# Expert output projection deferred by one turn with TensorE's order written out, and the adaptive-norm matmuls spread over four column groups, in a two-layer trunk with mixture-of-experts

## The chip, the cores and the metric

The kernel runs on one core of a Trainium2 chip. The metric is device time in microseconds of one execution, the median of several. TensorE has two clock levels, 1.2 and 2.4 GHz; the profile gives the granted clock of a stretch as a share of the higher one.

## The reference

Two layers over 1,024 tokens of width 1,024. Layer 0 mixes with a gated delta rule and a sparse attention, layer 1 with a gated linear attention; after each mixer stands a mixture of experts. What the change touches is this:

```python
mod = cond @ ada_w[layer] + ada_b[layer]          # cond = silu(c): 1 x 1024, ada_w[layer]: 1024 x 6144
sh_m, sc_m, gt_m, sh_f, sc_f, gt_f = jnp.split(mod, 6, axis=-1)
...
def expert_block(args):                            # 32 experts a layer, 2 per token
    xi, e = args
    hid = jax.nn.silu(xi @ w1[e]) * (xi @ w3[e])   # w1, w3: 1024 x 512
    return hid @ w2[e]                             # w2: 512 x 1024
```

## The kernel before

All values are float32. A large matmul is made of three (`mm3`, lines 112 to 114): each operand is split into a rounded part "hi" and the remainder "lo" (both of type fp32r), and hi·hi, lo·hi and hi·lo are added up in PSUM.

**Adaptive norm** (`ada_steps`, line 282). The 6,144 columns of a layer are made in three rounds of 2,048. A round has 16 tiles of 128 rows by 1,024 columns (512 KB each). `cond` stands in TensorE as a stationary operand 32 columns wide, so a matmul fills 32 of the 128 columns of the array, and `tile_position=(0, q)` says which. A round's PSUM tile holds four strips of 512 values at partitions 0, 32, 64 and 96. One tile feeds two of them: `u` says which pair, and each of its two matmuls has 512 columns. The first round (layer 0, columns 0 to 2,047) loads its weights as eight wide tiles on SP before anything else can run (`first`, line 448), and its tiles come in pairs. The other five rounds (80 tiles, `later`, line 470) are loaded on POOL's queue into two buffers and are taken one tile at a time between the steps of the input projection (matmuls `pj`).

**Mixture of experts** (`moe`, lines 1401 to 1665), once per layer. Up to 128 tokens of an expert are gathered from DRAM on POOL (`fetch_tokens`, line 1474), turned by TensorE (`tokens`, `tp<-xg`, line 1485), and split by ScalarE (`xh`, line 1487) and VectorE (`xl`, line 1488). `up` is 24 matmuls of 512 columns for `w1` and 24 for `w3`. `gated` makes `silu(p1) * p3` (`s`, `hd`, line 1505). `hidden` turns that (`tp<-hd`, line 142) and splits it (`hh` on ScalarE, line 1513; `hl` on VectorE, line 1514). `down` is another 24 matmuls in two halves `u`, copied out by ScalarE (line 1532) and scattered by POOL (line 1521).

A weight of 2 MB comes from DRAM as two pieces of 1 MB on SP's queue (line 1442), into six buffers `raw`. Each piece is rounded by ScalarE (`mhi`, line 1430), and its remainder is made by VectorE (`mlo`, line 1431). There are four buffers for such a pair, so two weights at a time. In `up` the first piece serves the first 12 matmuls and the second the last 12; in `down` each half `u` needs the first piece for six matmuls and the second for the next six.

The loop's body writes, for expert e: `up` by w3, `gated`, `up` of e+1 by w1, `hidden`, the tokens of e+2, `down` by w2, scatter. Each engine runs its instructions strictly in its own program's order. That order is chosen when the program is built, by a scheduler that weighs estimated times; it moves instructions of all engines past each other where the data allow. Every fourth expert `find_places` computes the token places of four later experts (`ix`, lines 1460 and 1464).

Of the kernel before, what the change touches and what calls it, by code (L numbers as in the profile page):

```python
# [9 lines left out]
F32 = mybir.dt.float32  # L10
# [12 lines left out]
P = 128  # L23
# [51 lines left out]
def run(gen):  # L75
    for _ in gen:
        pass
# [10 lines left out]
class Trunk:  # L88
# [175 lines left out]
    def ada_steps(self, rounds, wp, pp, load, wait):  # L264


        nc, cp = self.nc, self.cp
        n, total = 0, 2 * KD * len(rounds)
        w = load(0)
        for layer, g in rounds:  # L270
            bias = wp.tile([P, 512], F32, name="adab", bufs=1)
            for j in range(4):
                q = g * 4 + j
                nc.scalar.dma_start(bias[32 * j:32 * j + 32], bcast(self.d["ada_b"][layer, q * 512:(q + 1) * 512], 32))
# [16 lines left out]
            if g:  # L291
                for j in range(4):
                    q = g * 4 + j
                    nc.scalar.dma_start(self.mods[layer, q * 512:(q + 1) * 512][None, :], mr[32 * j:32 * j + 1])
# [5 lines left out]
            nc.vector.tensor_copy(col, pt.rearrange("p (c j r) -> p j c r", c=4, j=4)[:, :, :, 0])  # L300
            self.COL[layer, g] = col

    def ada_tile(self, i, rounds):

        (layer, g), (k, u) = rounds[i // (2 * KD)], divmod(i % (2 * KD), 2)
        c0 = g * 2048 + u * 1024
        return self.d["ada_w"][layer, k * P:(k + 1) * P, c0:c0 + 1024]
# [110 lines left out]
    def even_inproj(self):  # L418
# [29 lines left out]
        def first(i):  # L448
            k, u = divmod(i, 2)
            if u == 0:  # L450
                wide[k] = wp.tile([P, KD * W], F32, name="aw", tag="wlo" if k % 2 else "whi", bufs=2)[:, :2048]
                nc.sync.dma_start(wide[k], d["ada_w"][0, k * P:(k + 1) * P, :2048])
            return wide[k][:, u * 1024:(u + 1) * 1024]

# [949 lines left out]
    def moe(self, layer):  # L1404
        nc, tc, d = self.nc, self.tc, self.d
        tt, ts, stt, act, mm, tr = self.tt, self.ts, self.stt, self.act, self.mm, self.tr
        with ExitStack() as st:
# [38 lines left out]
            def places(n, R, val, iy, it):  # L1446
# [8 lines left out]
                tt(ob, in16[:, :, :, None].to_broadcast(b4), self.iob[:, None, None, :].to_broadcast(b4), op=OP.is_equal)  # L1455
                tt(oa, oa, val[:, :, :, None].to_broadcast(a4), op=OP.mult)
                p = pp.tile([P, 512], F32, name="ix", bufs=1)
# [4 lines left out]
                act(t, p[:8, :n * 16], AF.Copy)  # L1462
                p = pp.tile([P, 512], F32, name="ix", bufs=1)
                mm(p[:, :n * 16], self.to8[:8], t, start=True, stop=True)
# [13 lines left out]
            def tokens(xg):  # L1478
                xh = sp.tile([P, KD, P], F32R, name="xh", bufs=2)
                xl = sp.tile([P, KD, P], F32R, name="xl", bufs=2)  # L1480
                for u in range(2):
                    p = pp.tile([P, 512], F32, name="tp", bufs=2)
                    for c in range(4):
                        k = u * 4 + c
                        tr(p[:, c * P:(c + 1) * P], xg[:, k * P:(k + 1) * P], self.ident)  # L1485
                    us = slice(u * 4, u * 4 + 4)
                    act(xh[:, us], as4(p), AF.Copy)  # L1487
                    tt(xl[:, us], as4(p), xh[:, us].bitcast(F32), op=OP.subtract)  # L1488
                return xh, xl

# [43 lines left out]
            def find_places(e, n):  # L1534
                es = slice(e, e + n)
                places(n, self.R[:, :, es], self.val[:, :, es], yix[:, es], tix[:, es])

            def fetch_tokens(e):
                return gather(tix[:, e:e + 1], xgs[e % 2])

            find_places(0, 2)
            g = fetch_tokens(0)
# [5 lines left out]
            with tc.issue_after(self.turned[-1].ins), tc.issue_after(self.added[-1].ins), tc.issue_after(found.ins):  # L1548
                w3 = weights(0, "exp_w3")
            xt = {0: tokens(xgs[0])}  # L1550
            fetch_tokens(1)
            p1 = up(xt[0], w1)
            find_places(2, 2)
            xt[1] = tokens(xgs[1])
            fetch_tokens(2)
            scat = []
            for e in range(NE):
# [17 lines left out]
                scat.append(s)  # L1575
                if e == 1:
# [35 lines left out]
            def pick():  # L1612
# [11 lines left out]
                nc.vector.tensor_copy(xh, xv)  # L1624
                places(1, ri[:, :, None], xh[:, :, None], ixn[:, 0:1], ixn[:, 1:2])
                gather(ixn[:, 1:2], xgs[0])
# [21 lines left out]
            with tc.For_i(0, nv, 1) as _:  # L1648
                scatter(y, ixc[:, 0:1])
                for n in range(2, 6):  # L1650
                    fetch(n)
                x = tokens(xgs[0])
                w1 = take(0)
# [442 lines left out]
```

## Time and profile before

| | |
|---|---|
| median of 3 runs | 3092.82 us (3088.14 to 3100.25) |
| the profiled execution | 3102.59 us, of which the profile's span is 3100.9 us |
| TensorE (PE) busy | 2698.4 us (87%) |
| VectorE (DVE) busy | 2213.0 us (71%) |
| ScalarE (ACT) busy | 1690.7 us (55%) |
| GpSimd (POOL) busy | 514.8 us (17%) |
| DMA | 683.08 MB, mean 220 GB/s |

PE is the matrix engine, PEld its weight loads, SPq the queue of DMAs that SP issues. `out<-in` names the tiles that an instruction writes and reads. In the profile a matmul's end is modelled, so consecutive matmuls overlap in the rows; what one costs in a row of many is the distance between starts. L with a number is a line of the kernel.

### The profile page before, as it was taken

What the parts mean: (1) busy time and instruction counts of PE and PEld (TensorE: products, weight loads), DVE (VectorE), ACT (ScalarE), POOL (GpSimd) and SP (SyncE); (2) the same over time, 40 slices, a digit from 0 to 9 for tenths busy, and PEclk for the clock granted to TensorE, in tenths of its full rate; (3) what the DMA queues carried; (4) which work ended last, traced back from release to release, by engine and by line L of the source; (5) the groups of instructions that cost most, each with busy time, mean ns of one, the idle gap of its engine ahead of it and who ended that gap; (6) DMA issues with size and microseconds to landing.
All of it is one profiled execution on the core that took longest, in us unless ns stands there. A gap on an engine that the chain in (4) does not pass through costs nothing. (4 is left out here: it accounts for less than half of the span.)

```text
span 3100.9 us, 46537 instructions
## 1 busy us (share of the span) xinstructions
PE 2698.4 (87%) x17606; PEld 2142.8 (69%) x17606; DVE 2213.0 (71%) x4033; ACT 1690.7 (55%) x2191; POOL 514.8 (17%) x511
## 2 busy tenths in 40 slices
PE   5999999877997999999997479999997999999980
PEld 3566777756786777777775377888785777777760
DVE  6666668577867888778776563583578888777866
ACT  4456653232533776766764445355435767766662
POOL 1000111233201112212113310002001211121120
PEclk8999999888998999999998789999997999999995
DMA  6345665422125888898884532545555888888954
GB/s 222 95 126 170 186 186 149 126 93 64 64 96 190 323 335 333 336 356 337 322 315 182 187 134 92 170 145 164 188 190 192 326 335 337 334 337 345 341 216 172
DMA packets 228745, 683.08 MB, mean 220 GB/s; under 512 B 50261, under 2 KB 127369, under 8 KB 173994
## 3 DMA queue, kind: packets, MB, share of 16 engines
q1 hardware_dynamic: 160672, 548.14, 49.0%
q0 software_dynamic: 37424, 107.01, 10.1%
q10 hardware_dynamic: 30426, 24.97, 2.5%
q8 instruction: 138, 2.26, 0.3%
q14 instruction: 85, 0.70, 0.1%
HBM read 628.07 MB, written 94.40 MB: 233 GB/s over the span
## 5 line engine op out<-in xcount | busy, mean ns | idle before, releaser
L1431 DVE TENSOR_TENSOR mlo<-raw,mhi 128x2048 fp32r<-128x2048 f32 (+1 forms) x420 | 907.8, 2195 | 227.5 <-ACT mhi L1430 227.4
L1430 ACT ACTIVATE mhi<-raw 128x2048 fp32r<-128x2048 f32 (+1 forms) x420 | 757.9, 1840 | 126.9 <-PE h L114 76.7
L113 PE MATMUL h<-mlo,xh 128*128 128x512 f32 x1072 | 434.5, 405 | 17.7 <-DVE mlo L1431 17.4
L112 PE MATMUL h<-mhi,xh 128*128 128x512 f32 x1072 | 437.8, 408 | 5.5 <-ACT mhi L1430 2.8
L114 PE MATMUL h<-mhi,xl 128*128 128x512 f32 x1072 | 431.6, 403 | 0.1
L112 PE MATMUL pj<-whi,hh 128*128 128x256 f32 (+2 forms) x1088 | 323.3, 298 | 11.1 <-ACT hh L354 11.1
L114 PE MATMUL pj<-whi,hl 128*128 128x256 f32 (+2 forms) x1088 | 317.0, 292 | 3.4 <-DVE hl L355 3.4
L113 PE MATMUL pj<-wlo,hh 128*128 128x256 f32 (+2 forms) x1088 | 317.3, 292 | 1.4 <-DVE wlo L368 0.8
L112 PE MATMUL y<-mhi,hh 128*128 128x512 f32 x536 | 222.8, 416 | 71.6 <-ACT hh L1513 71.6
L113 PEld LDWEIGHTS h<-mlo,xh 128*128 128x128 f32 x1072 | 204.6, 191 | 82.2 <-DVE mlo L1431 33.0
L112 PEld LDWEIGHTS pj<-whi,hh 128*128 128x128 f32 x1088 | 209.8, 193 | 55.7 <-issue 26.2
L112 PEld LDWEIGHTS h<-mhi,xh 128*128 128x128 f32 x1072 | 206.4, 193 | 53.6 <-ACT xh L1487 3.8
L114 PEld LDWEIGHTS h<-mhi,xl 128*128 128x128 f32 x1072 | 205.1, 191 | 47.1 <-DVE xl L1488 1.0
L1474 POOL DMA_INDIRECT xg<-hbuf,tix x64 | 99.3, 1552 | 733.5 <-PE tp L1485 678.3
L114 PEld LDWEIGHTS pj<-whi,hl 128*128 128x128 f32 x1088 | 209.9, 193 | 10.9 <-DVE hl L355 4.7
L113 PE MATMUL y<-mlo,hh 128*128 128x512 f32 x536 | 216.4, 404 | 0.0
L113 PEld LDWEIGHTS pj<-wlo,hh 128*128 128x128 f32 x1088 | 210.6, 194 | 4.6 <-issue 1.6
L114 PE MATMUL y<-mhi,hl 128*128 128x512 f32 x536 | 212.9, 418 | 0.4 <-DVE hl L1514 0.3
L1521 POOL DMA_INDIRECT ybuf<-y,yix x64 | 152.2, 2378 | 305.1 <-ACT y L1532 291.6
L112 PEld LDWEIGHTS y<-mhi,hh 128*128 128x128 f32 x536 | 104.8, 195 | 106.1 <-ACT hh L1513 86.6
L1487 ACT ACTIVATE xh<-tp 128x512 fp32r<-128x512 f32 x134 | 79.0, 594 | 171.2 <-PE tp L1485 171.2
L1532 ACT ACTIVATE y<-y 128x512 f32<-128x512 f32 x134 | 78.9, 588 | 154.2 <-PE y L114 154.2
(715 smaller groups left out, 5169.1 us busy)
## 6 DMA issues: line engine op xcount, KB each, us to landing
raw<-in_exp_w_dram SPq DMA_DIRECT2D x380, 1024.0 KB
adaw<-in_ada_w_dram POOLq DMA_DIRECT2D x80, 512.0 KB, 4.1
yt<-ybuf SPq DMA_DIRECT2D x16, 1024.0 KB
wraw<-in_even_w_in_dram SPq DMA_DIRECT2D x48, 256.0 KB
x<-in_x_dram SPq DMA_DIRECT2D x16, 512.0 KB
aw<-in_ada_w_dram SPq DMA_DIRECT2D x8, 1024.0 KB
hbuf<-th SPq DMA_DIRECT2D x16, 512.0 KB
x<-x SPq DMA_DIRECT2D x16, 512.0 KB
```

Of the source, the lines that this page charges most:

```text
L112: self.mm(ps, ah, bh, start=first, stop=False)
L113: self.mm(ps, ah, bl, start=False, stop=False)
L114: self.mm(ps, al, bh, start=False, stop=last)
L1430: act(h[:, us], raw[:, us], AF.Copy)
L1431: (take[u] if take else tt)(l[:, us], raw[:, us], h[:, us].bitcast(F32), op=OP.subtract)
L1474: return nc.gpsimd.indirect_dma_start(out=xg, out_offset=None, in_=self.hbuf, in_offset=bass.IndirectOffsetOnAxis(ap=it, axis=0), bounds_c ...
L1487: act(xh[:, us], as4(p), AF.Copy)
L1521: return nc.gpsimd.indirect_dma_start(out=self.ybuf, out_offset=bass.IndirectOffsetOnAxis(ap=iy, axis=0), in_=y, in_offset=None, bounds_ch ...
L1532: act(y[:, u * 512:(u + 1) * 512], p, AF.Copy)
```

## The change

It has three parts. In the adaptive norm a tile's 1,024 columns now go to all four column groups, 256 columns each, and a round first makes the 256 left columns of each strip over all rows, then the right ones; bias, stored rows and the wide first tiles follow that layout. In the loop over experts, `down` of expert e-1 now stands between the two `up`s of turn e: its first half between the two halves of the token turning, its second behind them, and `hidden` of e behind that. And the loop's body is in a block that keeps TensorE's instructions in the order in which they are written; the other engines are still ordered by the scheduler. `find_places` yields twice, so that its two groups of matmuls stand before and after `up` by w1.

```diff
             ps = pp.tile([P, 512], F32, name="ada", bufs=1)
-            for k in range(KD):
-                for u in range(2):
+            for u in range(2):
+                for k in range(KD):
                     n += 1
                     ahead = load(n) if n < total else None
-                    for j in range(2):
-                        q = 32 * (2 * u + j)
-                        self.mm(ps[q:q + 32], self.cond[:, k], w[:, j * 512:(j + 1) * 512],
+                    for j in range(4):
+                        q = 32 * j
+                        self.mm(ps[q:q + 32, u * 256:(u + 1) * 256], self.cond[:, k], w[:, j * 256:(j + 1) * 256],
                                 start=(k == 0), stop=(k == KD - 1), tile_position=(0, q))
...
-            def down(h, w, y):
+            def down(h, w, y, halves=(0, 1)):
                 hh, hl = h
-                for u in range(2):
+                for u in halves:
...
+            def finish(e, h, w, y):
+                down(h, w, y, (1,))
                 s = scatter(y, yix[:, e:e + 1])
...
             for e in range(NE):
-                with tc.issue_after(g.ins) if e < 2 else nullcontext():
-                    p3 = up(xt.pop(e), w3 if e == 0 else weights(e, "exp_w3", q=late if e == 1 else early))
-                hd = gated(p1, p3)
-                if e + 1 < NE:
-                    p1 = up(xt[e + 1], weights(e + 1, "exp_w1"))
-                h = hidden(hd)
-                if e + 2 < NE:
-                    xt[e + 2] = tokens(xgs[e % 2])
-                if e % 4 == 0 and e + 4 < NE:
-                    find_places(e + 4, 4)
-                if e + 3 < NE:
-                    fetch_tokens(e + 3)
-                y = y_tile()
-                down(h, weights(e, "exp_w2"), y)
-                s = scatter(y, yix[:, e:e + 1])
+                with tc.manual_schedule(engines={mybir.EngineType.PE}):
+                    with tc.issue_after(g.ins) if e < 2 else nullcontext():
+                        p3 = up(xt.pop(e), w3 if e == 0 else weights(e, "exp_w3", q=late if e == 1 else early))
+                    hd = gated(p1, p3)
+                    new = tokens(xgs[e % 2]) if e + 2 < NE else iter(())
+                    if e + 2 < NE:
+                        xt[e + 2] = next(new)
+                    if before:
+                        y, w = y_tile(), weights(e - 1, "exp_w2")
+                        down(before, w, y, (0,))
+                    next(new, None)
+                    if e + 3 < NE:
+                        fetch_tokens(e + 3)
+                    if before:
+                        finish(e - 1, before, w, y)
+                    before = hidden(hd)
+                    found = find_places(e + 4, 4) if e % 4 == 0 and e + 4 < NE else iter(())
+                    next(found, None)
+                    next(found, None)
+                    if e + 1 < NE:
+                        p1 = up(xt[e + 1], weights(e + 1, "exp_w1"))
+                    run(found)
...
+            y, w = y_tile(), weights(NE - 1, "exp_w2")
+            down(before, w, y, (0,))
+            finish(NE - 1, before, w, y)
```

How this moves instructions, first on TensorE in the middle of layer 0's experts. Before, from the end of an `up` by w3 (`h`) over `hidden` to the first matmuls of `down` (`y`):

```order
L114 MATMUL h<-mhi,xl 128x512
L142 MATMUL tp<-ident,hd 128x128 x4
L1485 MATMUL tp<-ident,xg_10188 128x128 x4
L112 MATMUL h<-mhi,xh 128x512
L112 MATMUL y<-mhi,hh 128x512
L113 MATMUL y<-mlo,hh 128x512
L112 MATMUL y<-mhi,hh 128x512
L113 MATMUL y<-mlo,hh 128x512
L113 MATMUL h<-mlo,xh 128x512
```

Between the turning of `hd` and the matmuls that need it stand four transposes and one matmul. Now, at the end of `up` by w3 of an expert e:

```order
L114 MATMUL h<-mhi,xl 128x512
L1492 MATMUL tp<-ident,xg_10380 128x128 x4
L112 MATMUL y<-mhi,hh 128x512
L113 MATMUL y<-mlo,hh 128x512
L114 MATMUL y<-mhi,hl 128x512
L112 MATMUL y<-mhi,hh 128x512
L113 MATMUL y<-mlo,hh 128x512
L114 MATMUL y<-mhi,hl 128x512
L112 MATMUL y<-mhi,hh 128x512
```

These `y` are of expert e-1; its `hd` was turned before the 48 `up` matmuls that precede them. The first six need the first piece of w2, the seventh the second.

VectorE, in the turns of experts 1 to 11 of a layer (shown: expert 2). `raw_10924` and `raw_10930` are the two pieces of w2 of expert 1, `raw_10986` and `raw6_10992` those of w1 of expert 3; `hd` is of expert 2.

```order
L1436 TENSOR_TENSOR mlo_10927<-raw_10924,mhi_10926 128x2048
L1436 TENSOR_TENSOR mlo_10933<-raw_10930,mhi_10932 128x2048
L1436 TENSOR_TENSOR mlo_10989<-raw_10986,mhi_10988 128x2048
L1512 TENSOR_TENSOR hd_10912<-s1_10910,h_10885 128x128x4
L1436 TENSOR_TENSOR mlo_10995<-raw6_10992,mhi_10994 128x2048
```

Both remainders of w2 stand ahead of `hd`. In the turns of experts 12 to 31, 20 in each layer, the same engine has this order, where `raw_13075` and `raw_13081` are the pieces of w2, and `raw_13137` and `raw6_13143` those of w1:

```order
L1436 TENSOR_TENSOR mlo_13078<-raw_13075,mhi_13077 128x2048
L1512 TENSOR_TENSOR hd_13063<-s1_13061,h_13036 128x128x4
L1436 TENSOR_TENSOR mlo_13084<-raw_13081,mhi_13083 128x2048
L1495 TENSOR_TENSOR xl_13066<-tp_13067,xh_13065 128x512
L1436 TENSOR_TENSOR mlo_13140<-raw_13137,mhi_13139 128x2048
L1495 TENSOR_TENSOR xl_13066<-tp_13101,xh_13065 128x512
L1436 TENSOR_TENSOR mlo_13146<-raw6_13143,mhi_13145 128x2048
```

Here the remainder of w2's second piece has moved behind `hd`.

## Rows read from the trace of the kernel before

**Rows 1.** The page: busy time by engine, and two lines of the 40 slices.

```profile
PE 2698.4 (87%) x17606; PEld 2142.8 (69%) x17606; DVE 2213.0 (71%) x4033; ACT 1690.7 (55%) x2191; POOL 514.8 (17%) x511
...
PEclk8999999888998999999998789999997999999995
DMA  6345665422125888898884532545555888888954
```

**Rows 2.** Windows: length, busy us of PE, PEld, DVE, ACT, POOL; clock, DMA share, GB/s.

```profile
60.00:512.00 452.00, 440.73 (x2471) 311.77 (x2472) 311.42 (x858) 233.67 (x435) 48.08 (x93) 0.99 0.50 152
1030.00:1630.00 600.00, 562.52 (x2688) 447.34 (x2687) 487.44 (x350) 422.08 (x359) 116.58 (x60) 0.99 0.89 334
2390.00:2990.00 600.00, 562.07 (x2684) 448.58 (x2683) 484.05 (x353) 418.58 (x360) 115.34 (x58) 0.98 0.89 335
1320.00:1333.00 13.00, 11.62 (x56) 9.31 (x55) 8.78 (x7) 6.95 (x8) 1.02 (x1) 1.00 1.02 427
```

**Rows 3.** Waits in 1030 to 1630 us (PE, SP): us in total, times, longest.

```profile
PE y L112 <- ACT hh L1513: 31.4, 28, 1.4
PE h L113 <- DVE mlo L1431: 5.5, 14, 0.4
...
SPq L1442 <- DVE mlo L1431: 529.1, 176, 9.0
```

**Rows 4.** Groups on PE in 1030 to 1630 us: count, busy us, mean ns, idle before.

```profile
L112 PE MATMUL h<-mhi,xh 128*128 128x512 f32 x476 | 192.4, 404 | 0.0
...
L112 PE MATMUL y<-mhi,hh 128*128 128x512 f32 x232 | 95.9, 413 | 31.4 <-ACT hh L1513 31.4
...
L1485 PE MATMUL tp<-ident,xg 128*128 128x128 f32 x232 | 37.1, 285 | 0.0
L142 PE MATMUL tp<-ident,hd 128*128 128x128 f32 x120 | 18.0, 272 | 0.0
L1460 PE MATMUL ix<-ob,oa 128*8 128x16 f16 x200 | 6.1, 169 | 0.0
```

**Rows 5.** Timeline of one turn on PE and ACT: start, duration, instruction, idle before.

```profile
1311.84 0.39 PE L113 MATMUL h<-mlo,xh 128*128 128x512 f32 x1
...
1321.91 0.39 PE L114 MATMUL h<-mhi,xl 128*128 128x512 f32 x1
...
1322.14 0.60 PE L142 MATMUL tp<-ident,hd 128*128 128x128 f32 x4
...
1322.57 0.60 PE L1485 MATMUL tp<-ident,xg 128*128 128x128 f32 x4
...
1322.93 0.48 PE L112 MATMUL h<-mhi,xh 128*128 128x512 f32 x1
1324.15 0.58 ACT L1513 ACTIVATE hh<-tp 128x512 fp32r<-128x512 f32 x1
...
1324.79 0.50 PE L112 MATMUL y<-mhi,hh 128*128 128x512 f32 x1 [1.38 <-ACT hh L1513]
```

**Rows 6.** Groups on DVE and ACT in 1030 to 1630 us.

```profile
L1431 DVE TENSOR_TENSOR mlo<-raw,mhi 128x2048 fp32r<-128x2048 f32 x177 | 398.3, 2285 | 96.0 <-ACT mhi L1430 96.0
...
L1505 DVE TENSOR_TENSOR hd<-s,h 128x512 f32<-128x512 f32 x30 | 33.1, 1104 | 0.0
...
L1430 ACT ACTIVATE mhi<-raw 128x2048 fp32r<-128x2048 f32 x178 | 334.8, 1916 | 44.7 <-PE h L114 32.5 <-PE y L114 9.5 <-ACT mhi L1430 0.6
L1502 ACT ACTIVATE s<-h 128x512 f32<-128x512 f32 x29 | 17.4, 600 | 0.0
```

**Rows 7.** Adaptive norm on PE: the group in 60 to 512 us.

```profile
L282 PE MATMUL ada<-adaw,cond 128*32 128x512 f32 x320 | 86.2, 604 | 5.2 <-DMA adaw<-in_ada_w_dram 5.2
```

**Rows 8.** Timeline on PE: the first round's matmuls, and one later tile.

```profile
25.02 2.78 PE L282 MATMUL ada<-aw,cond 128*32 128x512 f32 x24
...
321.98 1.05 PE L282 MATMUL ada<-adaw,cond 128*32 128x512 f32 x4
322.97 0.39 PE L112 MATMUL pj<-whi,hh 128*128 128x260 f32 x1
```

More of the change, by code (lines that the diff above doesn't have):

```diff
@@ L271, in ada_steps @@
             bias = wp.tile([P, 512], F32, name="adab", bufs=1)
+            cols = "(u j c) -> j u c"
+            b2 = self.d["ada_b"][layer, g * 2048:(g + 1) * 2048].rearrange(cols, u=2, j=4)
             for j in range(4):
[L273 to L274 removed]
+                nc.scalar.dma_start(bias[32 * j:32 * j + 32].rearrange("p (u c) -> p u c", u=2), bcast(b2[j], 32))
             ps = pp.tile([P, 512], F32, name="ada", bufs=1)
[L276 to L277 removed]
+            for u in range(2):
+                for k in range(KD):
                     n += 1
                     ahead = load(n) if n < total else None
[L280 to L282 removed]
+                    for j in range(4):
+                        q = 32 * j
+                        self.mm(ps[q:q + 32, u * 256:(u + 1) * 256], self.cond[:, k], w[:, j * 256:(j + 1) * 256],
                                 start=(k == 0), stop=(k == KD - 1), tile_position=(0, q))
@@ L291, in ada_steps @@
             if g:
+                m2 = self.mods[layer, g * 2048:(g + 1) * 2048].rearrange(cols, u=2, j=4)
                 for j in range(4):
-                    q = g * 4 + j
-                    nc.scalar.dma_start(self.mods[layer, q * 512:(q + 1) * 512][None, :], mr[32 * j:32 * j + 1])
+                    nc.scalar.dma_start(m2[j][None], mr[32 * j:32 * j + 1].rearrange("p (u c) -> p u c", u=2))
                 continue
@@ L299, in ada_steps @@
             col = cp.tile([P, 4, 4], F32, name=f"col{layer}{g}")
-            nc.vector.tensor_copy(col, pt.rearrange("p (c j r) -> p j c r", c=4, j=4)[:, :, :, 0])
+            nc.vector.tensor_copy(col.rearrange("p (u a) (b c) -> p u (a b) c", u=2, c=2),
+                                  pt.rearrange("p (u c j r) -> p u j c r", u=2, c=2, j=4)[:, :, :, :, 0])
             self.COL[layer, g] = col
     def ada_tile(self, i, rounds):
-        (layer, g), (k, u) = rounds[i // (2 * KD)], divmod(i % (2 * KD), 2)
+        (layer, g), (u, k) = rounds[i // (2 * KD)], divmod(i % (2 * KD), KD)
         c0 = g * 2048 + u * 1024
@@ L448, in first @@
         def first(i):
[L449 to L453, printed above, removed]
+            n, v = divmod(i, 2)
+            if v == 0:
+                wide[n] = wp.tile([P, KD * W], F32, name="aw", tag="wlo" if n % 2 else "whi", bufs=2)[:, :2048]
+                u, k = divmod(i, KD)
+                nc.sync.dma_start(wide[n].rearrange("p (k c) -> p k c", k=2), d["ada_w"][0].rearrange("(k p) c -> p k c", p=P)[
+                    :, k:k + 2, u * 1024:(u + 1) * 1024])
+            return wide[n][:, v * 1024:(v + 1) * 1024]
         run(self.ada_steps([(0, 0)], ap_, pp, first, 0))
@@ L1456, in places @@
                 tt(oa, oa, val[:, :, :, None].to_broadcast(a4), op=OP.mult)
+                yield
                 p = pp.tile([P, 512], F32, name="ix", bufs=1)
@@ L1462, in places @@
                 act(t, p[:8, :n * 16], AF.Copy)
+                yield
                 p = pp.tile([P, 512], F32, name="ix", bufs=1)
@@ L1535, in find_places @@
                 es = slice(e, e + n)
-                places(n, self.R[:, :, es], self.val[:, :, es], yix[:, es], tix[:, es])
+                return places(n, self.R[:, :, es], self.val[:, :, es], yix[:, es], tix[:, es])
             def fetch_tokens(e):
                 return gather(tix[:, e:e + 1], xgs[e % 2])
-            find_places(0, 2)
+            run(find_places(0, 2))
             g = fetch_tokens(0)
@@ L1549, in moe, with all_tokens @@
                 w3 = weights(0, "exp_w3")
-            xt = {0: tokens(xgs[0])}
+            def all_tokens(xg):
+                for x in tokens(xg):
+                    pass
+                return x
+            xt = {0: all_tokens(xgs[0])}
             fetch_tokens(1)
             p1 = up(xt[0], w1)
-            find_places(2, 2)
-            xt[1] = tokens(xgs[1])
+            run(find_places(2, 2))
+            xt[1] = all_tokens(xgs[1])
             fetch_tokens(2)
             scat = []
-            for e in range(NE):
-                with tc.issue_after(g.ins) if e < 2 else nullcontext():
-                    p3 = up(xt.pop(e), w3 if e == 0 else weights(e, "exp_w3", q=late if e == 1 else early))
-                hd = gated(p1, p3)
-                if e + 1 < NE:
-                    p1 = up(xt[e + 1], weights(e + 1, "exp_w1"))
-                h = hidden(hd)
-                if e + 2 < NE:
-                    xt[e + 2] = tokens(xgs[e % 2])
-                if e % 4 == 0 and e + 4 < NE:
-                    find_places(e + 4, 4)
-                if e + 3 < NE:
-                    fetch_tokens(e + 3)
-                y = y_tile()
-                down(h, weights(e, "exp_w2"), y)
+            def finish(e, h, w, y):
+                down(h, w, y, (1,))
                 s = scatter(y, yix[:, e:e + 1])
@@ L1575, in moe @@
                 scat.append(s)
+            before = None
+            for e in range(NE):
+                with tc.manual_schedule(engines={mybir.EngineType.PE}):
[20 more added lines that the diff above has]
+                    run(found)
                 if e == 1:
@@ L1624, in pick @@
                 nc.vector.tensor_copy(xh, xv)
-                places(1, ri[:, :, None], xh[:, :, None], ixn[:, 0:1], ixn[:, 1:2])
+                run(places(1, ri[:, :, None], xh[:, :, None], ixn[:, 0:1], ixn[:, 1:2]))
                 gather(ixn[:, 1:2], xgs[0])
@@ L1651, in moe @@
                     fetch(n)
-                x = tokens(xgs[0])
+                x = all_tokens(xgs[0])
                 w1 = take(0)
```

2 lines of the change are left out of this document (1 added, 1 removed).

## The prediction

> **What bounds the kernel now.** I read the page first. TensorE is busy 87% of the span, VectorE 71%, and the DMA line stands at 8 or 9 tenths in two stretches only [rows 1]: the two runs through the experts. The windows give these stretches apart [rows 2]. In 600 us of either, TensorE is busy 562, VectorE 484 to 487, ScalarE 419 to 422, at 334 GB/s; in a stretch of 13 us without a pause the DMA moved 427 GB/s, so it has room. SP waited for buffers 529 of the 600 us [rows 3]: the loads are not late, the buffers come free late.
>
> So TensorE is nearest to its limit there, and the question is what it loses. From 1311.84 to 1321.91 lie 43 steps of 512-column matmuls, 0.234 us each; eight transposes take from 1322.14 to 1322.93, 0.1 us each [rows 5]. The stretch holds three lines of some 475 `up` matmuls and three of 232 `down` matmuls, 2,122 in all, and 352 transposes [rows 4]: 497 + 35 us. The places take 6.1 us [rows 4] and some 3 more for their second step (my estimate, half of the first). That makes 541; the other 59 us are lost, and 232 × 3 / 24 = 29 experts share them: **2.0 us per expert**. Where: `down` waits for `hh`, 31.4 us in 28 turns, and `up` for a remainder 5.5 us [rows 3]; the rest is turnaround around these and around the places. The timeline shows one: `hd` is turned at 1322.14, `hh` starts at 1324.15, `y` at 1324.79, and TensorE stood 1.38 us [rows 5].
>
> The third stretch is 60 to 512 us, the input projection of layer 0. TensorE is busy 441 of 452 us at a clock of 0.99, with VectorE at 311 [rows 2]: TensorE bounds it. The adaptive norm takes 86.2 us of it and waits 5.2 us for its tiles [rows 7].
>
> **The change, part by part.** The sum is made against the profiled execution, 3102.6 us; the median of the runs shown lies 9.8 us (0.3%) below it.
>
> *Column groups.* A float32 matmul shows as two records, so a later tile's two matmuls are four [rows 8]. They run as two batches of two: 1.05 us less the 0.60 of a single one [rows 7, 8] is 0.45 us from batch to batch. In the first round the tiles come in pairs and four records run at once: 24 records in 2.78 us are six batches, (2.78 - 0.60) / 5 = 0.44 us each [rows 8]. Four groups thus cost what two cost. With four matmuls of 256 columns a tile is two batches of four at half the length, 0.22 us: it saves 2 × 0.22 = 0.44 us, and 80 tiles 35 us, on the engine that bounds the stretch. Bounds: 0 if the four groups go two by two, 35 if all of it reaches the end. I take 28, near the upper end, since the row of the first round is the same operation with the same four groups; what I hold back is for tile loads, which already make TensorE wait 5.2 us [rows 7] and will be met earlier. The Trainium skill speaks against this piece ("TensorEngine Tiling (Array Packing)", section "Performance Considerations", "Instruction Overhead"): a matmul carries about 60 cycles of overhead, so a short dimension should not be cut further. By that the 320 added records would give back 8 us at 2.4 GHz or 16 at 1.2, estimates by that page; this piece would bring 12 to 20 us, and the sum below would be 3031 to 3039 instead of 3023. The trace does not show it: a batch of 512 columns takes the same 0.44 us whether two or four go at once [rows 8]. The first round itself already has four groups and the same bytes: nothing. Bias and stored rows are as many DMAs as before: nothing, and no one waits for them soon.
>
> *`down` one turn later.* The wait for `hh` goes: between `hidden` and the `down` that needs it now lie 48 matmuls, 11 us. What is late next is found from the orders shown above. In turns 1 to 11 VectorE has both remainders of w2 ahead of `hd`, and I find no wait: its work is 487 / 29 = 16.8 us per expert [rows 2] against 18.7 on TensorE (541 / 29). These turns gain the whole 2.0 us.
>
> In turns 12 to 31 the second remainder of w2 stands behind `hd`, and `hd` needs the last `up` matmul of w3. From that moment VectorE takes 1.10 us for `hd` and 2.29 for the remainder [rows 6], 3.39 us. TensorE meanwhile has four transposes, 0.4 us, and the six matmuls on the first piece, 6 × 0.234 = 1.4 [rows 5], and then stands, being now forbidden to do anything else: 3.39 - 1.8 = 1.6 us, and with two hand-overs between engines of some 0.1 us each (`hh` ends at 1324.73, `y` starts at 1324.79, rows 5) **1.8 us**. These 20 turns exchange a loss of 2.0 for one of 1.8.
>
> Per layer: 11 × 2.0 + 20 × 0.2 = 26 us. Two layers give 52. Bounds: 0 if the wait moves in all turns, 2 × 32 × 2.0 = 128 if it vanishes in all; I take 52, because the orders decide it turn by turn. The last expert's `down` now follows its own `hidden` with nothing between, as before, and costs the same one wait. Gathers: POOL now issues them behind the token turning of one turn, over a turn ahead of need; nothing waits. SP's loads keep a cycle of six pieces, rotated like their use.
>
> Sum: 3102.6 - 52 - 28 = 3022.6, or **3013** against the median.
>
> **The rivals.**
> - *No wait in the late turns.* If VectorE's remainder does not hold TensorE up, the gain is nearer 120 us: 3102.6 - 120 - 28 - 9.8 = 2945. Against it: `hd` cannot start before `up` ends, whatever else is early.
> - *The DMA becomes the bound.* 200 MB (334 GB/s for 600 us) for 29 experts at 18.7 us each is 370 GB/s, 87% of the 427 seen [rows 2]. If what can be held is 350, a turn takes 19.7 us: the early turns gain 1.0, 2 × (11 + 4) = 30, and the time is 3035.
> - *The column groups add nothing* (the change does not do what it says there): 3041.
> - *The wait moves in all turns* and only the column groups count: 3102.6 - 2 × 32 × 0.2 - 28 - 9.8 = 3052.
> - *Nothing counts*, both pieces being eaten by new waits: 3085 to 3100.
> - *Slower.* With the order fixed, TensorE stops at the first late thing. If the first remainder of w2 also comes after the `up`, because ScalarE can round it only when a buffer of w1 is free and `s` (0.60 us) is done, `hd` slips behind it: 1.10 + 2.29 - 0.4 = 3.0 us of standing, and then 2.29 - 1.4 = 0.9 more, 3.9 per turn instead of 2.0. Over 62 turns that is +118 - 28: 3183. It decides from a mean loss of 2.0 + 28 / 62 = 2.5 us per turn. Against it: from the end of `up` by w1 to the first remainder lie 0.60 + 1.92 + 2.29 = 4.8 us [rows 6], and `up` by w3 covers 5.6.
>
> **How the numbers follow.** The forecast (early turns free, late turns exchanged) has 0.55, with 2995 to 3032 as its own range from the 10 to 35 us of the column groups. No wait at all 0.08, DMA 0.11, no gain from column groups 0.08, wait moved everywhere 0.06, nothing 0.05, slower 0.07. The range 2970 to 3058 leaves out the first of these, the last two and little else. A measurement of this kernel can tell about 0.5%, 15 us, from no change. Faster by more than that (below 3077) are all but the last two: 0.88; within it 0.05; slower 0.07.
>
> **What would show it.** In the experts' stretches the wait of `y` on `hh` is gone; in its place stands `y` waiting for a remainder `mlo`, about 1.6 to 1.8 us at a time, some 20 times a layer and only from the twelfth turn on. Turns last about 18.7 us early and 20.5 late. The adaptive norm's later tiles show eight records of about 0.4 us each, with some 35 us less between starts, and the input projection ends some 28 us earlier. The forecast is wrong if the early turns keep 20 us, if the late ones fall to 18.7, or if the projection's end stays where it was.

## The result and the profile after

The changed kernel takes 3012.5 us (median of 4 runs, 3009.2 to 3014.5) against 3092.3 us before (4 runs, 3088.1 to 3100.3): a ratio of 0.9738 (95% interval 0.9716 to 0.976; the intervals below are of the same kind). The forecast was 3013. The number is right; the parts of the sum are less so, and they erred in opposite directions, as the runs below show. That the sum came out to the microsecond is luck.

The profiled execution of the changed kernel took 3010.9 us, near its median. That of the kernel before had taken 10 us more than its own, so the two spans differ by 91.8 us where the medians differ by 79.8. Stages are therefore compared one by one here, not spans.

The page of the changed kernel, against [rows 1]: the busy line of the engines, the clock and the DMA.

```profile
PE 2625.8 (87%) x17990; PEld 2119.4 (70%) x17990; DVE 2219.0 (74%) x4033; ACT 1686.1 (56%) x2191; POOL 498.3 (17%) x511
...
PEclk8999999898997999999999789999997999999995
DMA  6345664432124999999995532545554999999964
```

The 384 records more on PE (17,990 for 17,606) are the added matmuls of the column groups, 64 in the first round and 320 in the later tiles. DMA stands at 9 tenths in the experts' slices, where it stood at 8. The windows of the projection and of the two runs through the experts, against [rows 2] (length, busy us of PE, PEld, DVE, ACT, POOL; clock, DMA share, GB/s):

```profile
60.00:512.00 452.00, 430.64 (x2958) 333.85 (x2956) 336.15 (x904) 243.94 (x459) 50.46 (x98) 0.99 0.53 160
...
980.00:1580.00 600.00, 573.75 (x2816) 458.18 (x2815) 509.24 (x373) 435.46 (x374) 114.63 (x61) 1.00 0.94 346
2310.00:2910.00 600.00, 573.57 (x2823) 460.07 (x2822) 510.63 (x373) 435.78 (x375) 115.34 (x61) 0.99 0.95 345
```

In the experts more is done in 600 us: 2,816 records on PE for 2,688, TensorE busy 574 for 562. In the projection TensorE is busy *less* of the stretch, 431 of 452 us for 441: the work that was taken away has not all become time.

The waits of PE and SP in 980 to 1580 us, against [rows 3] (us in total, times, longest):

```profile
PE y L113 <- DVE mlo L1436: 23.2, 19, 1.7
PE tp L142 <- DVE xl L1495: 3.0, 1, 3.0
...
SPq L1447 <- DVE mlo L1436: 501.2, 172, 8.4
```

`y <- hh` (31.4 us, 28 times) is gone. `y <- mlo` is new: 19 times, and in 980 to 1210 us only once, at the end of that stretch, in the first late turn. The turns themselves are read from the starts of `hd`, one per expert (min/median/max in ns, first and last start in us). The kernel before from its first `hd` on, then the changed kernel's early and late turns:

```profile
L1505 DVE TENSOR_TENSOR hd<-s,h x30: 1097/1104/1119, 1012.3 to 1603.9; 128x512 f32<-128x512 f32 x30
```

```profile
L1512 DVE TENSOR_TENSOR hd<-s,h x13: 1076/1099/1118, 984.7 to 1206.6; 128x512 f32<-128x512 f32 x13
L1512 DVE TENSOR_TENSOR hd<-s,h x18: 1087/1091/1102, 1227.9 to 1566.9; 128x512 f32<-128x512 f32 x18
```

Before, 29 turns took 591.6 us, 20.4 each. Now 12 early turns take 221.9 us, 18.5 each, and 17 late ones 339.0 us, 19.9 each. The turn between, 21.3 us (1206.6 to 1227.9), is a late one that also computes places; late turns without places take 19.6, early ones 18.1. The first `hd` stands 27.6 us earlier.

The last matmul of the projection in layer 0 (`pj`) starts at 550.9 us, before at 575.6: 24.7 us earlier, where the prediction named some 28.

One late turn on PE and DVE (start, duration, instruction, idle before in brackets):

```profile
1327.37 0.40 PE L114 MATMUL h<-mhi,xl 128*128 128x512 f32 x1
1327.61 0.60 PE L1492 MATMUL tp<-ident,xg 128*128 128x128 f32 x4
1327.80 1.09 DVE L1512 TENSOR_TENSOR hd<-s,h 128x512 f32<-128x512 f32 x1 [0.89 <-PE h L114]
1327.96 0.48 PE L112 MATMUL y<-mhi,hh 128*128 128x512 f32 x1
...
1328.73 2.28 DVE L1436 TENSOR_TENSOR mlo<-raw,mhi 128x2048 fp32r<-128x2048 f32 x1
...
1329.20 0.39 PE L114 MATMUL y<-mhi,hl 128*128 128x512 f32 x1
1329.44 0.40 PE L112 MATMUL y<-mhi,hh 128*128 128x512 f32 x1
...
1331.07 0.50 PE L113 MATMUL y<-mlo,hh 128*128 128x512 f32 x1 [1.23 <-DVE mlo L1436]
```

This is the chain that the prediction worked out: the last `up` matmul of w3 starts at 1327.37, then come `hd`, then the remainder, and `y` goes on at 1331.07. TensorE has four transposes and seven matmuls of its own meanwhile and then stands. From 1329.44 to 1331.07 lie 1.63 us, where the next matmul should have come after 0.234: **1.40 us lost**, for 1.8 forecast. One matmul more was available than I counted: the first product with the second piece needs its rounded half only, not the remainder.

The chain of work that ended last, in 2550 to 2660 us of the second layer, names the same place in each late turn (three of them shown):

```profile
2558.80 2.30 DVE mlo L1436
...
2578.37 2.29 DVE mlo L1436
...
2617.53 2.29 DVE mlo L1436
```

Last the adaptive norm, against [rows 8]: one later tile and the matmul of the projection behind it.

```profile
301.89 0.64 PE L284 MATMUL ada<-adaw,cond 128*32 128x256 f32 x8
302.46 0.39 PE L112 MATMUL pj<-whi,hh 128*128 128x260 f32 x1
```

From the tile to the next matmul now lie 0.57 us, before 0.99 (321.98 to 322.97): 0.42 us less, for the 0.44 of the forecast. Over the 65 full tiles with a projection matmul behind them the median is 0.57 us too.

### The profile page after: what moved, and what is told of

It is laid out like the page before. It is cut to its first block, busy times and chain, and to the rows that moved or that the text cites. A ratio compares the mean times of both kernels' runs of the same rounds, so it can differ in the third digit from the quotient of the medians.

```text
span 3009.1 us, 47272 instructions
## 1 busy us (share of the span) xinstructions
PE 2625.8 (87%) x17990; PEld 2119.4 (70%) x17990; DVE 2219.0 (74%) x4033; ACT 1686.1 (56%) x2191; POOL 498.3 (17%) x511
## 5 line engine op out<-in xcount | busy, mean ns | idle before, releaser
L1481 POOL DMA_INDIRECT xg<-hbuf,tix x64 | 108.3, 1692 | 618.4 <-PE tp L1492 443.7
L1528 POOL DMA_INDIRECT ybuf<-y,yix x64 | 134.5, 2101 | 364.7 <-ACT y L1539 360.7
L113 PEld LDWEIGHTS y<-mlo,hh 128*128 128x128 f32 x536 | 101.3, 189 | 83.1 <-DVE mlo L1436 66.2
```

Source lines behind the costliest of these rows:

```text
L113: self.mm(ps, ah, bl, start=False, stop=False)
L1481: return nc.gpsimd.indirect_dma_start(out=xg, out_offset=None, in_=self.hbuf, in_offset=bass.IndirectOffsetOnAxis(ap=it, axis=0), bounds_c ...
L1528: return nc.gpsimd.indirect_dma_start(out=self.ybuf, out_offset=bass.IndirectOffsetOnAxis(ap=iy, axis=0), in_=y, in_offset=None, bounds_ch ...
```

## The experiments

The theory going in: the column groups bring some 28 us, the late `down` some 52, and the rest of the loss in the late turns is VectorE's order alone. Four runs came first, two that take the change apart and two that move VectorE's order.

**The column groups alone.** The kernel before with the adaptive norm of the changed one:

```diff
-                    for j in range(2):
-                        q = 32 * (2 * u + j)
-                        self.mm(ps[q:q + 32], self.cond[:, k], w[:, j * 512:(j + 1) * 512],
+                    for j in range(4):
+                        q = 32 * j
+                        self.mm(ps[q:q + 32, u * 256:(u + 1) * 256], self.cond[:, k], w[:, j * 256:(j + 1) * 256],
...
```

> The kernel before with the four column groups alone; the experts as before. Theory: each of the 80 later tiles takes 0.44 us less of TensorE and most of that reaches the end, so 28 us less than the kernel before, about 3064 us (3057 to 3072), and the first `hd` of layer 0 stands some 28 us earlier than the 1012 of the kernel before. Rival 1, the four groups bring nothing (they go two by two, or the tile loads take the gain): 3085 to 3100. Rival 2, each added matmul costs something of its own, so only 12 to 20 us: 3072 to 3080.

Measured: 3069.4 us, ratio 0.9939 (0.9919 to 0.9959), so 19 us less (13 to 25). The first `hd` is at 987.0 us, 25 earlier. A gain, and inside the theory's 3057 to 3072, but less than 28 and as near to the 12 to 20 us of the second rival; a later run measures that rival's price directly.

**The experts alone.** The changed kernel with the two column groups (the diff above, reversed).

> The changed kernel with the adaptive norm's two column groups of before; the experts as changed. Theory, the two pieces add up: 80 us of the whole change less 28, so 52 us less than the kernel before, about 3040 us (3030 to 3050), with the wait of `y` on `mlo` some 20 times a layer as in the changed kernel. Rival, the pieces overlap (the experts' gain needs the earlier start, or eats it): 3015 or 3060.

Measured: 3035.1 us, ratio 0.9829 (0.9811 to 0.9848), 53 us less (47 to 58), with the turns of the changed kernel. The two parts make 19 + 53 = 72 us, and the whole 81 (74 to 88): they add up as well as the intervals can tell.

**w2 ahead of `hd`.** VectorE must make both remainders of w2 before `hd`, in every turn:

```diff
-                    hd = gated(p1, p3)
+                    if before:
+                        y, w = y_tile(), weights(e - 1, "exp_w2")
+                    with tc.issue_after(self.low.ins) if before else nullcontext():
+                        hd = gated(p1, p3)
...
```

(`low` is the last remainder that was written.)

> The changed kernel, with VectorE's `hd` put behind both remainders of w2 in every turn. Theory, the late turns stand because the second remainder of w2 comes after `hd`, which needs the last `up` by w3: the wait of `y` on `mlo` (25 us and 20 times in the first layer's stretch) goes, and 20 turns of each layer fall from 19.6 to about 18.0 us, 60 to 68 us together: 2945 to 2955. Rival 1, the loads cannot go faster than now (a turn of 18.0 us is about 385 GB/s for every turn, where the stretch now holds 346): turns go to 19 us at best, 2985 to 3000, and the wait turns up at a DMA. Rival 2, ScalarE's rounding of w2, which still comes after `s`, makes `hd` late and the flip of `hd` waits in its place: 3005 to 3020.

Measured: 2956.4 us, ratio 0.9556 (0.9531 to 0.9581). In 980 to 1550 us PE has one wait left, the window shows TensorE busy to the end, and the starts of `hd` give late turns of 18.5 us (17 in 315.1):

```profile
PE tp L142 <- DVE xl L1495: 3.0, 1, 3.0
```

```profile
980.00:1550.00 570.00, 567.00 (x2809) 457.74 (x2808) 506.32 (x371) 434.57 (x373) 121.17 (x59) 1.00 0.97 362
```

```profile
L1512 DVE TENSOR_TENSOR hd<-s,h x18: 1072/1106/1114, 1231.4 to 1546.5; 128x512 f32<-128x512 f32 x18
```

So VectorE's order made the late turns long. The first rival falls: 362 GB/s, at a DMA share of 0.97, feed a TensorE that is busy 567 of 570 us. The second falls too: `hd` is later, but its flip (the turning by TensorE, `tp<-hd`) has the whole `down` in front of it.

**`hd` ahead of w2.** The opposite: the second remainder of w2 behind `hd` in all turns.

```diff
-                    (take[u] if take else tt)(l[:, us], raw[:, us], h[:, us].bitcast(F32), op=OP.subtract)
+                    with tc.issue_after(behind.ins) if behind else nullcontext():
+                        (take[u] if take else tt)(l[:, us], raw[:, us], h[:, us].bitcast(F32), op=OP.subtract)
...
```

(`behind` is the turn's `hd`, given for the second piece of w2 only.)

> The opposite of the kernel with w2 ahead: the second remainder of w2 is held behind `hd` in all turns. Theory: the 11 early turns of each layer get the wait of the late ones, 1.7 us and more, 22 x 1.7 = 37 us: about 3050 us (3045 to 3060), with some 31 waits of `y` on `mlo` a layer, and all turns near 19.6 us. Rival, the early turns are short for another reason than VectorE's order (a stock of loaded weights from the start of the layer that is used up): the waits appear but the time stays within 3005 to 3020.

Measured: 3056.5 us, ratio 0.989 (0.9866 to 0.9914). The early turns become late ones: 11 turns from 984.2 to 1204.2 us, 20.0 each, with the wait in nearly all:

```profile
PE y L113 <- DVE mlo L1437: 37.8, 29, 1.7
```

Both directions agree, and the early turns were not short because of a stock of weights.

**`down` late, TensorE's order free.** The changed kernel without the fixed order:

```diff
-                with tc.manual_schedule(engines={mybir.EngineType.PE}):
+                with nullcontext():
```

> The changed kernel without the fixed order of TensorE: `down` still comes one turn later, but the scheduler orders TensorE as in the kernel before. Theory, the late `down` carries the gain and the fixed order is worth little by itself: the late turns now reach `down` with one set of transposes fewer in front of it, so `y` waits up to 0.4 us longer in some 40 turns, 16 us at most: 3010 to 3030. Rival, the fixed order carries it: back to the column groups alone, 3060 to 3075.

Measured: 2969.4 us, ratio 0.9622 (0.9599 to 0.9644). Neither expectation holds: it is **some 40 us faster than the changed kernel** (43 by the medians, 36 by the ratios). One half of the change had been working against the other. VectorE still makes `hd` before the second remainder, but the scheduler had ordered TensorE otherwise:

```profile
1471.68 0.63 PE L112 MATMUL y<-mhi,hh 128*128 128x512 f32 x2
1471.88 1.10 DVE L1512 TENSOR_TENSOR hd<-s,h 128x512 f32<-128x512 f32 x1 [1.32 <-PE h L114]
...
1472.83 2.28 DVE L1436 TENSOR_TENSOR mlo<-raw,mhi 128x2048 fp32r<-128x2048 f32 x1
...
1474.73 0.40 PE L112 MATMUL y<-mhi,hh 128*128 128x512 f32 x1
1475.16 0.50 PE L113 MATMUL y<-mlo,hh 128*128 128x512 f32 x1
```

From 1471.68 to 1474.73 it goes through *both* column halves of `down` as far as the first piece of w2 and the rounded half of the second carry it (14 matmuls), and only then needs the late remainder, for which it stands 0.43 - 0.23 = 0.20 us. The fixed order goes through one half with both pieces and reaches it after seven. My expectation had counted the transposes that move away and had not looked at the order inside `down`.

**First pieces first, order fixed.** That makes a new theory, and this run tests it: the fixed order stays, and `down` is written as both halves by the first piece, then both by the second.

```diff
-                for u in halves:
-                    p = pp.tile([P, 512], F32, name="y", bufs=2)
-                    for k in range(4):
-                        hi, lo = w[k // 2]
...
+                for i in pieces:
+                    for u, p in enumerate(ps):
+                        for k in (2 * i, 2 * i + 1):
+                            hi, lo = w[i]
```

> The changed kernel with its fixed order, but within `down` both column halves go by the first piece of w2 before either goes by the second (VectorE's order in the late turns stays: second remainder behind `hd`). Theory, the fixed order of the changed kernel costs only because 6 matmuls and 4 transposes, 1.8 us, stand between the last `up` and the second piece; now 12 matmuls and 8 transposes do, 2.8 + 0.8 = 3.6 us against VectorE's 3.4 and two hand-overs: the waits of `y` on `mlo` go or fall under 0.3 us, turns of 18.0 to 18.4 us, 2950 to 2970. Rival, a fixed order loses whatever stands inside `down` (the loads or ScalarE are held up): 2985 to 3012.

Measured: 2969.7 us, ratio 0.9613 (0.958 to 0.9646), the same as with the free order. Of the wait in 980 to 1580 us this is left, and the late turns are 18.7 us (17 in 317.4, those with places included):

```profile
PE y L113 <- DVE mlo L1436: 0.5, 2, 0.3
```

```profile
L1512 DVE TENSOR_TENSOR hd<-s,h x18: 1081/1092/1102, 1231.1 to 1548.5; 128x512 f32<-128x512 f32 x18
```

So in the late turns it is not that the order is fixed, but which order was written: halves outside, pieces inside. The two kernels come to the same time by different ways, though: with the free order the first turn of a layer takes 13.1 us (20.3 with the fixed one), while its turns of experts 12 to 15 take 20 to 21 before they settle at 18.5.

**The fixed order without the late `down`.** Column groups, and the loop as it was written before, with TensorE held to that order throughout:

```diff
+            with tc.manual_schedule(engines={mybir.EngineType.PE}):
...
-            for e in range(NE):
+                for e in range(NE):
...
```

> The column groups and a fixed order of TensorE, without the late `down`: the whole loop over experts in the order in which it is written (w3, w1 of the next, the flip of `hd`, tokens, places, `down` of the same expert). Theory, the wait for `hh` comes back in every turn (some 1.4 us, as in the kernel before) and the fixed order takes little away from that: 3045 to 3085, with `y` waiting for `hh` some 30 times a layer. Rival, the fixed order by itself brings the gain: 3035 or less.

Measured: 3328.3 us, ratio 1.0757 (1.0731 to 1.0784), far outside both. The wait is not the one I named. The waits in 980 to 1580 us, the windows ahead of one such wait and behind it, and its timeline:

```profile
PE tp L1490 <- DVE hl L1519: 95.6, 24, 4.1
```

```profile
1310.00:1321.00 11.00, 11.00 (x49) 8.83 (x48) 10.72 (x6) 8.32 (x7) 2.45 (x1) 1.00 0.67 216
...
1326.00:1330.00 4.00, 4.00 (x12) 3.32 (x13) 1.12 (x2) 0.60 (x1) 1.02 (x1) 0.50 1.01 420
```

```profile
1321.22 0.60 PE L1490 MATMUL tp<-ident,xg 128*128 128x128 f32 x4
1322.93 2.29 DVE L1436 TENSOR_TENSOR mlo<-raw,mhi 128x2048 fp32r<-128x2048 f32 x1 [0.51 <-ACT mhi L1435]
...
1325.14 0.68 DVE L1519 TENSOR_TENSOR hl<-tp,hh 128x512 fp32r<-128x512 f32 x1
...
1325.88 1.11 PE L1490 MATMUL tp<-ident,xg 128*128 128x128 f32 x4 [4.06 <-DVE hl L1519]
```

There are two buffers `tp` in PSUM. The flip of `hd` takes one and the first half of the tokens the other; the second half needs the first one back, and its reader `hl` stands on VectorE behind remainders of weights. TensorE stands 4.06 us and then runs at 0.50 of its clock, the lower of its two levels, until about 1330.6. Turns take 24.0 us. With the late `down` the flip comes last ahead of 48 `up` matmuls, and from the second turn on the same two buffers hold nobody up.

**128 columns.** Each matmul of 256 columns in the adaptive norm as two of 128, so that another 640 records stand in the later tiles:

```diff
-                        self.mm(ps[q:q + 32, u * 256:(u + 1) * 256], self.cond[:, k], w[:, j * 256:(j + 1) * 256],
-                                start=(k == 0), stop=(k == KD - 1), tile_position=(0, q))
+                        for v in range(2):
+                            c0 = j * 256 + v * 128
+                            self.mm(ps[q:q + 32, u * 256 + v * 128:u * 256 + v * 128 + 128], self.cond[:, k], w[:, c0:c0 + 128],
+                                    start=(k == 0 and v == 0), stop=(k == KD - 1 and v == 1), tile_position=(0, q))
```

> The changed kernel with each of the adaptive norm's matmuls of 256 columns as two of 128: 768 matmuls more in all, of them 640 records and more in the later 80 tiles. Theory, a matmul has hardly a price of its own here (a tile went from 1.19 to 0.78 us between the neighbouring matmuls, 0.03 us short of the 0.44 that no price at all would give, so some 8 ns for each of the four added records): 80 tiles with eight more records at 8 ns are 5 us, 3010 to 3025. Rival, each has a price of 25 to 50 ns: 640 of them 16 to 32 us, 3028 to 3045, and a tile of 1.0 us or more.

Measured: 3020.0 us, ratio 0.9763 (0.9742 to 0.9784), inside the theory's 3010 to 3025; its interval overlaps that of the changed kernel, so the times alone give no price. A tile shows it directly:

```profile
303.29 0.67 PE L286 MATMUL ada<-adaw,cond 128*32 128x128 f32 x16
303.89 0.39 PE L112 MATMUL pj<-whi,hh 128*128 128x260 f32 x1
```

To the next matmul lie 0.60 us where eight records took 0.57: 4 ns for each added record, some 2 us over 80 tiles. The Trainium skill ("TensorEngine Tiling (Array Packing)", section "Performance Considerations", "Instruction Overhead") gives each matmul an overhead of about 60 cycles; at 2.4 GHz that is 25 ns, an estimate by that page. The tile does not show it for each record. If four records run side by side, the 0.03 us are 15 ns for each of two added rounds of four, so some overhead for each round is not excluded.

**Half of the adaptive norm's products.** The column groups save some 34 us on TensorE, and the projection ends 25 earlier. Where do the other 9 go? This kernel leaves every second of the later tiles out of the sum, 40 of 80:

```diff
+                        if (layer or g) and k % 2:
+                            continue
...
```

> The changed kernel without every second of the adaptive norm's later tiles in the sum (40 of the 80 tiles are loaded but not multiplied; the weights of the adaptive norm, and what is routed after them, are other numbers, so only the time up to the first `hd` of layer 0 is read, 985 to 989 us in the runs with the column groups, 993 once). It takes 40 x 0.78 = 31 us more from TensorE. Theory, behind the column groups TensorE has caught up with VectorE at the end of the projection (in 340 to 500 us it waits 4.5 us for `qa` and 2.6 for `col`, where the two column groups waited for neither): less than half of it arrives, the first `hd` at 972 to 985. Rival, TensorE still bounds the projection and the gain that is missing went elsewhere: 25 to 31 us, the first `hd` at 956 to 963.

Measured, in one execution: the last matmul of the projection starts at 545.5 us, where the changed kernel has 550.9, so some 5 of the 31 us arrive there. The first `hd` is at 988.6 us, inside the 984 to 993 us of the kernels with column groups: so far down nothing of the 31 can be seen. The waits in 340 to 500 us, of the changed kernel and then of this one:

```profile
PE tp L606 <- DVE qa L498: 4.5, 3, 3.1
PE ada L284 <- DVE col L302: 2.6, 1, 2.6
PE ada L284 <- DMA adaw<-in_ada_w_dram: 1.0, 2, 0.6
```

```profile
PE tp L608 <- DVE qa L500: 4.0, 3, 2.9
PE pj L113 <- DVE wlo L373: 4.0, 1, 4.0
PE ada L286 <- DVE col L304: 3.5, 1, 3.5
```

TensorE now meets VectorE's results early, one after the other; loads hardly count in this stretch (0.9 us here). Its clock falls too, as the windows of 460 to 500 us show, the changed kernel first (before, it was 1.00 there; with the column groups alone 0.96):

```profile
460.00:500.00 40.00, 35.79 (x294) 29.94 (x293) 37.15 (x74) 4.61 (x14) 4.17 (x9) 0.91 0.56 168
```

```profile
460.00:500.00 40.00, 33.62 (x241) 31.36 (x241) 31.89 (x51) 6.59 (x15) 1.40 (x4) 0.85 0.47 146
```

So at the projection's end the theory holds in kind, with less than half arriving, and the rival falls. The first `hd` came later than even the theory's 972 to 985. What bounds the stretch from the projection to that `hd` is not shown; it scatters from kernel to kernel by as much as is missing here.

**The order free, w2 ahead.** The kernel with w2 ahead, and the fixed order taken away.

> The kernel with w2 ahead of `hd` (2956 us), without the fixed order of TensorE. Theory, once no remainder is late nothing is left for a fixed order to prevent: within 0.5% of it, 2945 to 2970. Rival, TensorE then again turns tokens or places in front of what is needed first and `hd` is late: 2975 to 3010.

Measured: 2962.7 us, ratio 0.9588 (0.9568 to 0.9608), within 0.5% of 2956.4, as the theory has it: without a late remainder the fixed order neither costs nor brings much on the whole. Turn by turn it does both. In layer 0 the free order saves 6.0 us in the first two turns (32.5 for 38.5) and loses 6.9 in those of experts 11 to 16 (119.8 for 112.9).

**The first turn free.** The kernel with w2 ahead, its fixed order only from the second turn on:

```diff
-                with tc.manual_schedule(engines={mybir.EngineType.PE}):
+                with tc.manual_schedule(engines={mybir.EngineType.PE}) if e else nullcontext():
```

> The kernel with w2 ahead of `hd` (2956 us), with the first turn of each layer left to the scheduler. Theory, at the head of a layer the fixed order stops TensorE at tokens whose gather has not landed (8.3 us in the second layer of the changed kernel), and the first five turns take 94.7 us against 88.8 where all turns are free: 6 us a layer, about 2945 us (2938 to 2950). Rival, the head's wait only moves to the next turn: 2953 to 2962.

Measured: 2947.2 us, ratio 0.9545 (0.9514 to 0.9576), the fastest kernel of all, some 60 us below the changed one (65 by the medians, 60 by the ratios). Its interval overlaps that of the kernel with w2 ahead (0.9531 to 0.9581), so the times alone don't show the 9 us between their medians. The starts of `hd` in layer 0 do: to the 31st it takes 551.6 us, where the kernel with w2 ahead takes 557.4 (989.1 to 1546.5), and the first turn is 13.1 us.

```profile
L1512 DVE TENSOR_TENSOR hd<-s,h x31: 1078/1106/1119, 989.2 to 1540.8; 128x512 f32<-128x512 f32 x31
...
L1512 DVE TENSOR_TENSOR hd<-s,h x2: 1107/1110/1112, 989.2 to 1002.3; 128x512 f32<-128x512 f32 x2
```

The time came as expected, but the mechanism is not the one I gave. The 8.3 us for a gather stand ahead of the first `hd`, outside the fixed block. What holds the first turn up in the changed kernel is this, on its timeline:

```profile
984.75 1.08 DVE L1512 TENSOR_TENSOR hd<-s,h 128x512 f32<-128x512 f32 x1
985.67 2.27 DVE L1436 TENSOR_TENSOR mlo<-raw,mhi 128x2048 fp32r<-128x2048 f32 x1
987.87 1.26 DVE L1495 TENSOR_TENSOR xl<-tp,xh 128x512 fp32r<-128x512 f32 x2
988.59 0.66 PE L142 MATMUL tp<-ident,hd 128*128 128x128 f32 x4 [3.01 <-DVE xl L1495]
```

It is the wait of the fixed order without the late `down` once more: the flip of `hd` needs a buffer `tp` back from the tokens, whose reader `xl` stands behind a remainder. In all other turns `down` lies between the two; the first has none yet. With that turn free, PE has no wait left in 975 to 1007 us. Of the 7.2 us that the first turn gets shorter, 1.2 come back in the second (19.4 for 18.2), and 6 remain.

## Why the prediction was right, and where it was not

**TensorE bounds the experts, and the `hh` wait is the loss: right.** With the waits gone TensorE is busy 567 of 570 us, and an early turn without places takes 18.1 us: 72 matmuls of 0.234 and 12 transposes of 0.1 are 18.05.

**Early turns gain 2.0 each: right.** Leaving out the first turn, which has no `down` in it and took 20.3 us, eleven turns end at 1206.6: 201.6 / 11 = 18.3 for 20.4, a gain of 2.1 each and 23 us a layer, for 22.

**Late turns exchange 2.0 for 1.8: right in kind, the size off.** The wait, its two engines, its 20 times and the twelfth turn came as said. It costs 1.4 us for two reasons: the seventh matmul (0.23 us) needs no remainder, and the remainder starts 0.93 us behind the start of `hd` (1327.80 to 1328.73), where 1.10 were counted. From 1206.6 to 1566.9 lie 18 late turns of 20.0 us, a gain of 0.4 each and over 19 turns 8 us a layer, for 4.

**The ends of the loop: missed.** I held that the last expert's `down` costs what it cost before, and looked at no cost at the head. But the first turn now has one `down` less, 24 matmuls or 5.6 us, that returns behind the last `hd`; that is even only if the first turn gets shorter. It did not, with 20.3 us, because the fixed order stands there for `xl`, while it takes 13.1 us where it is free. The next `hd` behind the loop of layer 0 comes 38.4 us after the last expert's, before 33.4, so 5 us of the 5.6 are seen there.

So a layer gains 23 + 8 - 6 = 25 us for the forecast's 26, out of errors that cancel by luck: 5 too little in the turns, 6 too much at the ends. From the first `hd` of layer 0 to that next `hd` behind its loop it took 666.1 us and takes 639.8, 26 less. The experts alone measured 53 us (47 to 58) for 52.

**The column groups bring 28: too high, and for the wrong reason.** The term on TensorE was right, 0.42 us a tile for 0.44, 34 us in 80. What I held back, 7 us for tile loads, was too little and the wrong thing: in 340 to 500 us loads cost 1.0 us of waiting, VectorE's `qa` (a tile that TensorE turns) and `col` (the finished columns of a round) 7.1, and the clock in 460 to 500 was 0.91 here and 0.96 in the kernel with column groups alone, before 1.00. The prediction read VectorE's 311 of 452 us as room; but a share over a stretch says nothing of the moments in which a result is awaited. About 25 us reach the projection's end and the first `hd`, 19 (13 to 25) the end of the kernel, an interval that reaches up to those 25.

**The 9.8 us between profile and median: not a property of the kernel.** The changed kernel's profile lies at its median. Taking them off was needed all the same, since that one profile was 10 us too long. As much lies where the change touches nothing: from the first `hd` behind the experts of layer 0 to the first of layer 1 that execution took 701 us and the changed kernel 690; the kernel with TensorE's order free took 700, so executions differ there whatever the kernel.

**The rivals.** *No wait in the late turns* (2945) was not this kernel, but it is what w2 ahead of `hd` makes of it: 2956, and 2947 with the first turn free. Its arithmetic was good, and it shows what the change left behind. *The DMA bound* at 350 GB/s: 362 to 366 were held. *Column groups add nothing* (3041): alone they bring 19 us. *The wait moves in all turns* (3052): the kernel that puts `hd` ahead makes that happen, 3056.5. *Slower*, because a fixed order stops at the first late thing: not here, but the fixed order without the late `down` is just that, at the buffers `tp`, 8% slower.

**What I didn't see at all** is that the order as it was written cost some 40 us against a free one. The prediction wrote that TensorE is "now forbidden to do anything else" and priced the standing, but took the order inside `down` as given, and did not ask what the late turns would be if it were free.

## What to carry to other kernels

When an order is written out by hand, put first, among pieces that are ready, everything that uses the early piece, and then what uses the late one: here two loops exchanged in `down` were worth some 40 us. Price a deferral at its ends too, since the first turn is emptier and the last one fuller. And an engine that was the bound of a stretch is the bound of only some of its moments: after the first gain, look for the engine that it now meets, before counting the second.

## What was not expected of the hardware

After a stand of 4.06 us (the fixed order without the late `down`) TensorE was granted 0.50 of its clock, 1.2 GHz, from 1326 to 1330 us: matmuls of 512 columns then started 0.43 us apart instead of 0.234, and the first at the old pace began at 1330.63. After the 3.01 us in the first turn of the changed kernel the clock was 0.70 on average in 989 to 993 us: from 990.67 to 993.23 matmuls started 0.43 us apart. The late turn shown above, with its 1.40 us, left it at 1.00 in 1329 to 1333 us. So a long wait cost more than it lasted: 4.1 us of standing there, and from 1325.88 to 1330.63 some 2 us of slow running behind it (four transposes and nine matmuls, 2.5 us at the old pace, took 4.75).

The loads held 362 to 366 GB/s over 570 us, at a DMA share of 0.97 to 0.98, without TensorE waiting for a weight: more than the 350 at which the prediction had put the doubtful limit.
